# Two-layer diffusion trunk on one core: attention stages and delayed sums placed by a clock of the engines kept while the program is written

## The chip, the cores and the metric

The kernel runs on one core of one Trainium2 chip. The core has TensorE (PE, matrix products into PSUM banks), VectorE (DVE), ScalarE (ACT), GpSimd (POOL) and DMA queues; the queue that brings the weights is issued from SyncE (SP). Each engine takes its own instructions strictly in order and waits at an instruction until its operands are there, so the order in which the program is written decides who waits. The metric is the device time of one execution in microseconds.

## What is computed

Two layers over 256 latent tokens and 256 context tokens of width 1024. Of the reference, cut to what matters:

```python
mx = (silu(c) @ w_ada[l] + b_ada[l]).reshape(bsz, 9, 1, d)     # nine modulation vectors
mc = (silu(c_ctx) @ w_ada[l] + b_ada[l]).reshape(9, d)         # the same of the context
x = x + 0.5 * mx[2] * swiglu(modulate(rmsnorm(x, g[0]), mx[0], mx[1]), w_ffn1_in, w_ffn1_out)
hx = modulate(rmsnorm(x, g[1]), mx[3], mx[4])
p = hx @ w_in                                                   # queries, keys, values, gates
o_a = differential_attention(...)   # 4 heads, "a"
o_b = gated_linear_attention(...)   # 4 heads, both directions, chunks of 64, "b"
o_c = windowed_attention(...)       # 8 heads on 2 key heads, sink logit, "c"
x = x + mx[5] * ((ga*(o_a @ w_br_a) + gb*(o_b @ w_br_b) + gc*(o_c @ w_br_c)) @ w_out)
x = x + 0.5 * mx[8] * swiglu(modulate(rmsnorm(x, g[2]), mx[6], mx[7]), w_ffn2_in, w_ffn2_out)
```

The context goes the same way with `mc`, in layer 1 only as far as the latent tokens read it. The result is the RMS-normed latent stream.

## The kernel before

**Weights.** Every weight is loaded once, 512 KB to a `Unit`, into one of 6 raw buffers `wr`. `split_unit` parts it into a high half `wh` (ACT copies it) and a low half `wl` (DVE subtracts), in a ring of 4 pairs. A product is then three matmuls in place of one: high by high, low by high, high by low (`mm3`, line 112). Activations lie as columns, 512 of them (both streams) in layer 0 and the first FFN of layer 1, 256 in what follows. Nearly all PE work is such a product of `fm_units` (line 411): a unit has two or more *parts*, and a part is a run of 12 matmuls into one bank of PSUM.

**The order.** The program is one flat list that the loop at lines 1380 to 1399 walks. At each part it adds one to `n_part`, first puts in what `later` (line 345) delayed by so many parts, then the part's matmuls, then with `ahead()` the loads and splits that have become possible, and at the end of a unit the work on its result.

**Modulation vectors.** Sixteen vectors (seven of layer 0, all nine of layer 1) are made beside an FFN. `mixed` puts one of eight loads of `w_ada` behind each FFN unit. `ada_step` (line 280) multiplies it on DVE by a column of `sc` into four accumulators `s_t` (two for the last four vectors, of which the context has no use): line 291 for k = 0, line 293 for k = 1 to 7. After k = 7, `later(..., 4)` delays `ada_sum` (line 297) by four parts. `ada_sum` sums each accumulator over its partitions on PE: 32 (or 16) small matmuls against the constant `pick`. `ada_done` then transposes the sums on DVE (line 263) and adds the bias. The two vectors of layer 0 that its first FFN needs are made by matmuls alone and are not touched.

**Mixers.** An attention is a list of items, each a list of stages. An item of "a" or "c" has `s0` (scores, softmax), `s1` (transposes of the probabilities), `s2` (product with the values), and in "a" `s3` (head norm, `finish_head`, line 797: a square on ACT in `s2`, then a sum over partitions by a matmul with `ones_d`, logarithm and exponential on ACT, multiplication on DVE, split into halves). The linear attention has `decay` items ("B", two stages) and `head` items ("b", four stages, with the recurrence over chunks, line 125, in `s1`, and `finish_head` in `s3`). `turns(items, lags)` (line 1010) makes turns of a fixed pattern: turn t holds stage s of item t - lags[s], late stages first. `spread` (line 1069) strews the turns over the parts of the mixer's projections by weights, and at "need a", "need c", "need b", ahead of the first product that reads that attention's result `oh`, it puts in all the turns that are left. Order of groups: a, c, B, b.

Of the kernel before, what the change touches and what calls it, by code (L numbers as in the profile page):

```python
# [16 lines left out]
D = 1024  # L17
# [18 lines left out]
N_SLOT = 69  # L36

LAGS_A0 = (0, 2, 4, 5)
LAGS_C0 = (0, 2, 3)
WEIGHTS0 = (1.0, 1.0, 0.8, 2.0)  # L40
LAGS_A1 = (0, 2, 4, 5)
LAGS_C1 = (0, 2, 3)
# [3 lines left out]
class Ring:  # L46


    def __init__(self, pool, n, prefix):
        self.pool, self.prefix, self.count = pool, prefix, 0  # L50
        self.free = deque(f"{prefix}{i}" for i in range(n))
        self.n = n
        self.low = n
        self.held = {}

    def get(self, dtype=F32, shape=(128, 512)):
# [5 lines left out]
        self.held[id(t)] = (t, tag)  # L62
        return t

# [25 lines left out]

def f32(ap):
    return ap.bitcast(F32)
# [3 lines left out]
def trunk_kernel(ctx: ExitStack, tc: tile.TileContext, a: dict, out: bass.AP, dbg=None):  # L96
# [8 lines left out]
    S = Ring(sp, N_SLOT, "s")  # L105
    P = Ring(pp, 8, "p")


    def mm(o, l, r, start=True, stop=True):
        nc.tensor.matmul(o, l, r, start=start, stop=stop)  # L110
# [7 lines left out]
    def act(o, i, f, **kw):  # L118
        nc.scalar.activation(out=o, in_=i, func=f, **kw)  # L119

    def tt(o, x, y, op):
        nc.vector.tensor_tensor(out=o, in0=x, in1=y, op=op)  # L122

    def stt(o, x, s, y, op0, op1):
        nc.vector.scalar_tensor_tensor(out=o, in0=x, scalar=s, in1=y, op0=op0, op1=op1)  # L125
# [5 lines left out]
    def col(v, name):  # L131
        t = const.tile([128, 1], F32, name=name)
        nc.vector.memset(t, v)
# [12 lines left out]
    nc.vector.memset(ones_d, 1.0 / D)  # L146
    sc = const.tile([128, KD, 32], F32, name="sc")
    nc.vector.memset(sc, 0.0)
    pick = const.tile([128, 2, 32], F32, name="pick")
    nc.vector.memset(pick, 0.0)  # L150
    for s in range(2):
        nc.vector.memset(pick[:, s, s:s + 1], 1.0)
# [14 lines left out]
    def first_loads():  # L167
        cr = raw["c"] = S.get()
        nc.sync.dma_start(out=cr[0:8, 0:128], in_=a["c"].rearrange("o (k p) -> (o k) p", p=128))
        nc.scalar.dma_start(out=cr[8:16, 0:128], in_=a["c_ctx"].rearrange("(k p) -> k p", p=128))  # L170
        nc.scalar.dma_start(out=kf[:, C_ID:C_ID + 128], in_=a["k_f"][:, C_ID:C_ID + 128])
        for l in range(DEPTH):
            r = raw["rows", l] = S.get()
            nc.gpsimd.dma_start(out=r[24:96, 0:128], in_=a["b_ada"][l].rearrange("(k p) -> k p", p=128))
            nc.gpsimd.dma_start(out=r[0:24, 0:128], in_=a["norm_g"][l].rearrange("n (k p) -> (n k) p", p=128))
            nc.gpsimd.dma_start(out=r[96:97, 0:128], in_=a["diff_subln"][l:l + 1, :])
            nc.gpsimd.dma_start(out=r[97:98, 0:128], in_=a["gla_norm"][l:l + 1, :])
            nc.gpsimd.dma_start(out=r[98:106, 0:128], in_=a["final_g"].rearrange("(k p) -> k p", p=128))
# [26 lines left out]
    def tokens(k):  # L205
# [3 lines left out]
        for t in range(4):  # L209
            nc.tensor.transpose(ps[:, t * 128:(t + 1) * 128], raw["t", half, t][:, j * 128:(j + 1) * 128], ident)  # L210
        xt[k] = S.get()
        if k % 2:
            nc.vector.tensor_copy(out=xt[k], in_=ps)
# [7 lines left out]
    def side_loads():  # L221

        nc.sync.dma_start(out=kf[:, 0:C_ID], in_=a["k_f"][:, 0:C_ID])
        for l in range(DEPTH):
            nc.sync.dma_start(out=sink[:, l, :], in_=a["swa_sink"][l:l + 1, :].to_broadcast([128, 8]))
            lp = S.get()
            nc.sync.dma_start(
# [7 lines left out]
            nc.vector.tensor_reduce(out=s, in_=pr, axis=AX.X, op=ALU.add)  # L235
# [25 lines left out]
    def ada_done(l, i, ps, b0=0, nb=KD, streams_=2):  # L261
        tr = S.get()
        nc.vector.transpose(out=tr[:, 0:32 * nb], in_=ps[:, 0:32 * nb])
# [11 lines left out]
        elif i in (2, 8):  # L275
            nc.vector.tensor_scalar_mul(out=m, in0=m, scalar1=0.5)
# [3 lines left out]
    def ada_step(l, i, k, w):  # L280
# [13 lines left out]
        if k == KD - 1:  # L294
            later(lambda: ada_sum(l, i, ns), 4)
# [1156 lines left out]
```

## Time and profile before

| | us |
|---|---|
| median of 3 runs | 2268.08 (2267.97 to 2269.63) |
| the profiled execution, its own time | 2268.44 |
| its span, first to last instruction | 2266.3 |
| PE busy | 2201.1 (97% of the span) |
| DVE busy | 1418.5 (63%) |
| ACT busy | 990.5 (44%) |
| mean granted clock of PE | 0.989 of full speed |

The profiled execution lies 0.4 us above the median and 2.1 us lie outside its span. PE is the engine that is nearly always busy; DVE and ACT have room on the mean, but each is a link in chains that PE waits for. A busy PE may still run at its lower clock, so idle time and granted clock are read together.

### The profile page before, as it was taken

How to read it: one execution, taken by the hardware profiler on the slowest of the kernel's cores; microseconds unless marked ns; L12 is line 12 of the kernel's file. 1: busy time of each engine (PE TensorE's matmuls, PEld its weight loads, DVE VectorE, ACT ScalarE, POOL GpSimd, SP SyncE). 2: the span in 40 equal slices, each digit the busy share in tenths (PEclk: the TensorE clock that was granted, in tenths of full speed). 3: DMA queues.
4: the chain of work that ended last, by engine and by line, in shares of the span. 5: the costliest groups of instructions: out<-in, count | busy, mean ns of one | idle time of the engine just before them, and what ended most of it. 6: DMA issues, size and time to landing. Idle time of an engine off the chain costs nothing.

```text
span 2266.3 us, 32253 instructions
## 1 busy us (share of the span) xinstructions
PE 2201.1 (97%) x12903; PEld 1883.1 (83%) x12903; DVE 1418.5 (63%) x2432; ACT 990.5 (44%) x1701; POOL 17.3 (1%) x40
## 2 busy tenths in 40 slices
PE   7999999998999999999999999999999799998998
PEld 5888888976887788888888898888897688998998
DVE  5677788766465665678776565333366655877655
ACT  4321223666566444432222242222347567664443
POOL 0000000000000000000000000000000000000000
PEclk9999999999999999999999999999999999999999
DMA  8566565331222123356656534333234123356652
GB/s 310 163 188 190 182 193 186 107 88 54 67 65 75 56 66 100 115 167 190 195 183 189 164 123 146 99 97 94 83 96 121 57 84 113 113 164 200 215 185 94
DMA packets 246645, 304.47 MB, mean 134 GB/s; under 512 B 12874, under 2 KB 218180, under 8 KB 246496
## 3 DMA queue, kind: packets, MB, share of 16 engines
q1 hardware_dynamic: 245472, 301.65, 43.1%
q8 instruction: 101, 1.65, 0.3%
q10 hardware_dynamic: 448, 0.59, 0.1%
q14 instruction: 48, 0.39, 0.1%
q0 software_dynamic: 576, 0.18, 0.0%
HBM read 298.19 MB, written 4.19 MB: 133 GB/s over the span
## 4 chain that ended last, share of the span: by engine, by line
PE 84%; DVE 6%; ACT 6%; issue 1%; DMA 1%; SPq 0%; ACTq 0%; DVEq 0%
PE p_t L110 83%; ACT s_t L119 5%; DVE wl L122 2%; DVE s_t L122 1%; DVE s_t L125 1%; ACT wh L119 1%; PE p_t L699 1%; DMA s_t<-in_w_ada_dram 1%; DVE av_s L757 1%; DVE s_t L764 0%; DMA x<-s_t 0%; DVE cv_s L837 0%; SPq L185 0%; DVE av_s L763 0%; PE p_t L623 0%
## 5 line engine op out<-in xcount | busy, mean ns | idle before, releaser
L110 PE MATMUL p_t<-s_t,wh 128*128 128x512 f32 (+1 forms) x6152 | 1638.8, 353 | 2.4 <-ACT wh L119 2.2
L110 PEld LDWEIGHTS p_t<-s_t,wh 128*128 128x128 f32 x6152 | 1086.9, 189 | 171.0 <-issue 9.6
L110 PE MATMUL p_t<-s_t,wl 128*128 128x512 f32 (+2 forms) x3076 | 1046.0, 352 | 0.8 <-DVE wl L122 0.8
L122 DVE TENSOR_TENSOR wl<-wr,wh 128x1024 fp32r<-128x1024 f32 (+2 forms) x423 | 479.1, 1139 | 501.9 <-ACT wh L119 501.1
L119 ACT ACTIVATE wh<-wr 128x1024 fp32r<-128x1024 f32 (+2 forms) x423 | 414.9, 988 | 638.4 <-PE p_t L110 304.0
L110 PEld LDWEIGHTS p_t<-s_t,wl 128*128 128x128 f32 (+1 forms) x3076 | 582.0, 189 | 79.6 <-DVE wl L122 1.3
L119 ACT ACTIVATE s_t<-s_t 128x512 fp32r<-128x512 f32 (+5 forms) x338 | 185.2, 548 | 341.0 <-DVE s_t L122 230.9
L110 PE MATMUL p_t<-s_t,s_t 128*128 128x256 f32 (+4 forms) x2040 | 278.2, 304 | 21.4 <-ACT s_t L119 16.9
L119 ACT ACTIVATE s_t<-p_t 128x512 f32<-128x512 f32 (+6 forms) x464 | 219.3, 490 | 166.5 <-PE p_t L110 103.8
L110 PEld LDWEIGHTS p_t<-s_t,s_t 128*128 128x128 f32 (+2 forms) x2040 | 233.8, 187 | 52.6 <-ACT s_t L119 23.0
L122 DVE TENSOR_TENSOR s_t<-s_t,s_t 128x512 fp32r<-128x512 f32 (+5 forms) x315 | 181.8, 578 | 141.2 <-ACT s_t L119 137.7
L293 DVE SCALAR_TENSOR_TENSOR s_t<-wr,sc,s_t 128x512 f32<-128x512 f32 x392 | 269.0, 746 | 0.0
L122 DVE TENSOR_TENSOR s_t<-s_t,p_t 128x512 f32<-128x512 f32 (+1 forms) x144 | 85.0, 591 | 28.9 <-PE p_t L110 22.2
L110 PE MATMUL p_t<-wh,s_t 128*128 128x512 f32 x256 | 83.7, 399 | 2.8 <-ACT wh L119 2.8
L125 DVE SCALAR_TENSOR_TENSOR s_t<-s_t,mods,s_t 128x256 fp32r<-128x256 f32 (+1 forms) x176 | 70.6, 477 | 10.3 <-ACT s_t L119 10.3
L125 DVE SCALAR_TENSOR_TENSOR s_t<-p_t,mods,s_t 128x256 f32<-128x256 f32 x136 | 60.9, 478 | 21.7 <-PE p_t L110 21.5
L110 PEld LDWEIGHTS p_t<-wh,s_t 128*128 128x128 f32 x256 | 49.3, 193 | 13.3 <-ACT wh L119 3.0
L110 PE MATMUL p_t<-wl,s_t 128*128 128x512 f32 x128 | 51.0, 399 | 0.5 <-DVE wl L122 0.5
L119 ACT ACTIVATE s_t<-p_t,av_s 128x512 f32<-128x512 f32 (+1 forms) x48 | 29.2, 615 | 30.6 <-DVE av_s L758 30.6
L119 ACT ACTIVATE s_t<-s_t,mods 128x256 fp32r<-128x256 f32 x88 | 36.4, 497 | 12.0 <-DVE s_t L125 12.0
L119 ACT ACTIVATE s_t<-s_t,one 128x512 f32<-128x512 f32 (+1 forms) x64 | 40.4, 631 | 2.1
L699 PE MATMUL p_t<-kf,s_t 128*128 128x128 f32 x240 | 36.0, 282 | 0.0
(98 smaller groups left out, 629.7 us busy)
## 6 DMA issues: line engine op xcount, KB each, us to landing
wr<-in_w_ffn_in_dram SPq DMA_DIRECT2D x176, 512.0 KB, 4.3
wr<-in_w_ada_dram SPq DMA_DIRECT2D x128, 512.0 KB, 4.5
wr<-in_w_mix_in_dram SPq DMA_DIRECT2D x108, 512.0 KB, 3.7
wr<-in_w_ffn_out_dram SPq DMA_DIRECT2D x80, 512.0 KB, 3.6
s_t<-in_w_ada_dram SPq DMA_DIRECT2D x32, 256.0 KB, 6.2
wr<-in_w_mix_out_dram SPq DMA_DIRECT2D x16, 512.0 KB, 3.5
wr<-in_w_ffn_out_dram SPq DMA_DIRECT2D x16, 256.0 KB, 2.8
wr<-in_w_br_a_dram SPq DMA_DIRECT2D x8, 512.0 KB, 3.5
```

The lines of the kernel that those rows point to most:

```text
L110: nc.tensor.matmul(o, l, r, start=start, stop=stop)
L119: nc.scalar.activation(out=o, in_=i, func=f, **kw)
L122: nc.vector.tensor_tensor(out=o, in0=x, in1=y, op=op)
L125: nc.vector.scalar_tensor_tensor(out=o, in0=x, scalar=s, in1=y, op0=op0, op1=op1)
L293: eng.scalar_tensor_tensor(out=o, in0=x, scalar=c, in1=o, op0=ALU.mult, op1=ALU.add)
L699: nc.tensor.transpose(pt[:, 128 * t:128 * t + 128], p[:, 128 * t:128 * t + 128], ident)
L757: nc.vector.tensor_reduce(out=v[:, m:m + 1], in_=ps[m][:, 0:nk], axis=AX.X, op=ALU.max)
```

## The change

The fixed turns go. While the program is written, a `Clock` keeps for each engine a time up to which it is taken, and for each tile when it will be there; each engine is wrapped in a `Timed` that books every instruction that goes through it. The costs booked are constants of the code. `later` now takes the tiles that the delayed work waits for and puts it in at the first part at which they are there by that clock (or after 12 parts). The sixteen `ada_sum` go into a deque of their own, `sums`, under the same rule with the accumulators as tiles and 40 parts at most. Mixer items are in a `Group`: at each part a stage goes in if its operands are there, the PSUM banks that it takes are empty and three slots are free; a new `s0` also wants DVE and ACT less than 4.0 us behind. `spread` now only releases items at places given by the same weights, each group a few empty places (`IDLE`) before its "need", and at "need" `Group.finish` puts in whatever stages are left, at once. What an instruction is, and how often it runs, stays the same on every engine.

In `ada_step` the line `eng = nc.vector` (line 387 of the changed kernel) is as it was, not `DVEe`: these products go past the clock.

```diff
-LAGS_A0 = (0, 2, 4, 5)
-LAGS_C0 = (0, 2, 3)
+LATE = 2
+SLACK = 4.0
+
+IDLE = {"a": 5, "c": 3, "B": 1, "b": 3}
...
+    def empty(self, n):
+
+        return len(self.free) >= n and all(
+            self.clock.used.get(b, 0.0) <= self.clock.now["PE"] for b in list(self.free)[:n])
...
         if k == KD - 1:
-            later(lambda: ada_sum(l, i, ns), 4)
+            sums.append((lambda: ada_sum(l, i, ns), tuple(x for a_ in acc for x in a_), "PE", n_part + 40))
...
+    def later(f, *wait, eng="PE", most=12):
+
+        put_off.append((f, wait, eng, n_part + most))
+
+    def is_there(tiles, eng="PE"):
+        return not tiles or clock.at(*tiles) <= max(clock.now["PE"], clock.now[eng])
+
+    def behind(eng):
+        return clock.now[eng] - clock.now["PE"]
+
+    def due():
+        for q in (put_off, sums):
+            while q:
+                f, wait, eng, most = q[0]
+                if n_part < most and not (is_there(wait, eng) and behind("DVE") < SLACK):
+                    break
+                q.popleft()[0]()
+        for g in list(live):
+            g.step()
...
+    class Group:
...
+        def step(self, force=False):
...
+            for i in range(self.begun):
+                s = self.at[i]
+                if s == len(self.items[i]) or i and self.at[i - 1] <= s:
+                    continue
+                f, wait, banks = self.items[i][s]
+                if not force:
+                    if not is_there(wait() if wait else ()) or not P.empty(banks) or len(S.free) < 3:
+                        continue
+                    late = self.begun - i > LATE
+                    if s == 0 and not (fresh and (late or behind("DVE") < SLACK and behind("ACT") < SLACK)):
+                        continue
+                f()
+                self.at[i] += 1
...
+        def finish(self):
+            self.begun = len(self.items)
+            while not self.over:
+                self.step(True)
...
-            todo = deque((g, t, wt) for g, (ts, wt) in groups.items() for t in ts)
+            todo = deque()
+            for name, (g, idle, wt) in groups.items():
+                todo.extend((name, g.start if i < len(g.items) else lambda: None, wt) for i in range(len(g.items) + idle))
...
+                        out_.append(groups[g][0].finish)
...
-            "a": (and_then(turns(a_items(), lags_a), free_a), weights[0]),
+            "a": (Group(a_items(), free_a), IDLE["a"], weights[0]),
...
         elif p[0] == "part":
             n_part += 1
-            while put_off and put_off[0][0] < n_part:
-                put_off.popleft()[1]()
+            due()
```

The order moves at two kinds of places. The first is each of the sixteen sums. On PE, around the sum of layer 1's vector 0 (`pick` rows; `p_t`... `wh` rows are an FFN's products), the rows before are:

```order
L110 MATMUL p_t359_9183<-s_t639_8173,wh153_9095 128x512
L110 MATMUL p_t359_9183<-s_t642_8178,wh153_9095 128x512
L110 MATMUL p_t361_9239<-s_t684_8860,pick_83 32x128 x4
L110 MATMUL p_t361_9239<-s_t686_8862,pick_83 32x128 x4
L110 MATMUL p_t361_9239<-s_t685_8861,pick_83 32x128 x4
L110 MATMUL p_t361_9239<-s_t687_8863,pick_83 32x128 x4
L110 MATMUL p_t360_9196<-s_t632_8162,wh153_9095 128x512
```

The sum stands between the two parts of `wh153`. After, the same stretch of PE's queue is:

```order
L159 MATMUL p_t358_9112<-s_t639_8173,wh151_9017 128x512
L159 MATMUL p_t358_9112<-s_t642_8178,wh151_9017 128x512
L159 MATMUL p_t359_9183<-s_t685_8881,pick_83 32x128 x4
L159 MATMUL p_t359_9183<-s_t687_8883,pick_83 32x128 x4
L159 MATMUL p_t359_9183<-s_t686_8882,pick_83 32x128 x4
L159 MATMUL p_t359_9183<-s_t688_8884,pick_83 32x128 x4
L159 MATMUL p_t360_9203<-s_t620_8142,wh152_9055 128x512
```

The sum stood inside the products of `wh153`; now it stands at the end of those of `wh151`, three parts of 12 matmuls earlier. On DVE, the same sum: the last products into the accumulators (L293, in the changed kernel L393, with wr234), then splits and the transpose of the sum, the rows before are:

```order
L122 TENSOR_TENSOR s_t700_9168<-s_t696_9085,s_t699_9167 128x512
L293 SCALAR_TENSOR_TENSOR s_t684_8860<-wr234_9051,sc_81,s_t684_8860 128x512
L293 SCALAR_TENSOR_TENSOR s_t685_8861<-wr234_9051,sc_81,s_t685_8861 128x512
L293 SCALAR_TENSOR_TENSOR s_t686_8862<-wr234_9051,sc_81,s_t686_8862 128x512
L293 SCALAR_TENSOR_TENSOR s_t687_8863<-wr234_9051,sc_81,s_t687_8863 128x512
L122 TENSOR_TENSOR wl155_9180<-wr241_9177,wh155_9179 128x1024
L291 TENSOR_SCALAR s_t701_9209<-wr236_9091,sc_81 128x512
L291 TENSOR_SCALAR s_t702_9210<-wr236_9091,sc_81 128x512
L291 TENSOR_SCALAR s_t703_9211<-wr236_9091,sc_81 128x512
L291 TENSOR_SCALAR s_t704_9212<-wr236_9091,sc_81 128x512
L122 TENSOR_TENSOR wl156_9222<-wr243_9219,wh156_9221 128x1024
L263 STREAM_TRANSPOSE s_t706_9256<-p_t361_9239 128x256
```

Behind the last products come the next vector's first four, two splits, and only then the transpose. After, DVE's rows from the same gate product on are:

```order
L159 TENSOR_TENSOR s_t700_9168<-s_t696_9085,s_t699_9167 128x512
L393 SCALAR_TENSOR_TENSOR s_t685_8881<-wr234_9051,sc_81,s_t685_8881 128x512
L393 SCALAR_TENSOR_TENSOR s_t686_8882<-wr234_9051,sc_81,s_t686_8882 128x512
L393 SCALAR_TENSOR_TENSOR s_t687_8883<-wr234_9051,sc_81,s_t687_8883 128x512
L393 SCALAR_TENSOR_TENSOR s_t688_8884<-wr234_9051,sc_81,s_t688_8884 128x512
L159 TENSOR_TENSOR wl155_9180<-wr241_9177,wh155_9179 128x1024
L159 STREAM_TRANSPOSE s_t701_9200<-p_t359_9183 128x256
L159 TENSOR_TENSOR mods1_90<-s_t701_9200,cols1_88 128x16
L391 TENSOR_SCALAR s_t702_9229<-wr236_9091,sc_81 128x512
```

The products into the accumulators keep their place behind the FFN's gate (the first row); the transpose moved up past the next vector's first products and one split.

The second kind is the mixers. On PE, at the end of layer 1's mixer, ahead of the first product of the third branch (`wh317`), which reads all heads' results, the rows before are:

```order
L110 MATMUL p_t641_17159<-s_t917_13719,wh316_17033 128x256
L110 MATMUL p_t641_17159<-s_t920_13724,wh316_17033 128x256
L110 MATMUL p_t641_17159<-s_t923_13729,wh316_17033 128x256
L110 MATMUL p_t641_17159<-s_t926_13734,wh316_17033 128x256
L110 MATMUL p_t642_17216<-s_t1160_16771,wh317_17089 128x256
L110 MATMUL p_t642_17216<-s_t1160_16771,wl317_17090 128x256
```

The branch stands behind a projection's products and nothing else. After, PE's rows ahead of the same branch are:

```order
L159 MATMUL p_t638_17161<-s_t1065_15401,s_t1131_16325 128x128
L159 MATMUL p_t639_17162<-s_t1065_15401,s_t1131_16325 128x128
L159 MATMUL p_t640_17194<-s_t1181_17171,s_t1059_15341 128x128 x2
L159 MATMUL p_t640_17194<-s_t1039_15107,s_t1182_17176 128x64 x2
L159 MATMUL p_t640_17194<-s_t1181_17171,s_t1060_15349 128x128 x2
L159 MATMUL p_t640_17194<-s_t1039_15107,s_t1182_17176 128x64 x2
L159 MATMUL p_t641_17205<-s_t1184_17203,ones_d_79 128x256
L159 MATMUL p_t642_17216<-s_t1163_16867,wh317_17002 128x256
L159 MATMUL p_t642_17216<-s_t1163_16867,wl317_17003 128x256
```

Before, the last head was through 48 projection matmuls ahead of the branch; after, its stages `s1` (p_t638, p_t639), `s2` (p_t640) and `s3` (`ones_d`) stand directly ahead of the branch, put in by `Group.finish`.

## Rows read from the trace of the kernel before

**Rows 1.** The page: busy time and instructions by engine; the chain that ended last.

```profile
PE 2201.1 (97%) x12903; PEld 1883.1 (83%) x12903; DVE 1418.5 (63%) x2432; ACT 990.5 (44%) x1701; POOL 17.3 (1%) x40
...
PE 84%; DVE 6%; ACT 6%; issue 1%; DMA 1%; SPq 0%; ACTq 0%; DVEq 0%
```

**Rows 2.** Waits of PE over the span: us in total, times, longest us.

```profile
PE p_t L110 <- ACT s_t L119: 29.3, 17, 5.9
...
PE p_t L653 <- ACT s_t L119: 3.6, 2, 2.6
```

**Rows 3.** Stretches: us, busy (x instructions) by engine, granted clock, DMA share, GB/s.

```profile
1000.00:1250.00 250.00, 250.00 (x1250) 205.22 (x1249) 187.94 (x272) 65.94 (x78) 0.00 (x0) 1.00 0.62 192
...
1450.00:1500.00 50.00, 50.00 (x222) 41.43 (x221) 17.22 (x22) 10.77 (x11) 0.00 (x0) 1.00 0.33 100
...
2112.00:2140.00 28.00, 28.00 (x236) 28.00 (x235) 16.74 (x23) 12.49 (x18) 0.00 (x0) 1.00 0.67 213
...
470.00:600.00 130.00, 116.36 (x571) 93.03 (x571) 77.50 (x157) 81.94 (x181) 2.71 (x5) 0.96 0.23 66
1714.00:1990.00 276.00, 254.09 (x1771) 221.66 (x1770) 185.34 (x390) 177.87 (x365) 4.96 (x13) 0.97 0.33 97
```

**Rows 4.** Timeline of DVE: start, duration, [idle before]; last products of four vectors.

```profile
115.04 2.73 DVE L293 SCALAR_TENSOR_TENSOR s_t<-wr,sc,s_t 128x512 f32<-128x512 f32 x4
...
382.96 2.74 DVE L293 SCALAR_TENSOR_TENSOR s_t<-wr,sc,s_t 128x512 f32<-128x512 f32 x4
...
1062.03 0.69 DVE L122 TENSOR_TENSOR s_t<-s_t,s_t 128x512 fp32r<-128x512 f32 x1 [0.70 <-ACT s_t L119]
1062.64 2.73 DVE L293 SCALAR_TENSOR_TENSOR s_t<-wr,sc,s_t 128x512 f32<-128x512 f32 x4
...
2107.71 1.41 DVE L293 SCALAR_TENSOR_TENSOR s_t<-wr,sc,s_t 128x512 f32<-128x512 f32 x2
```

**Rows 5.** Timeline of PE: the sums of the same four vectors.

```profile
123.34 1.08 PE L110 MATMUL p_t<-s_t,pick 128*32 128x128 f32 x32
...
386.42 1.08 PE L110 MATMUL p_t<-s_t,pick 128*32 128x128 f32 x32
...
1068.06 1.08 PE L110 MATMUL p_t<-s_t,pick 128*32 128x128 f32 x32
...
2110.58 0.65 PE L110 MATMUL p_t<-s_t,pick 128*32 128x128 f32 x16
```

**Rows 6.** Timeline of PE: first and last of nine waits of 1.98 us or more.

```profile
26.29 2.08 PE L110 MATMUL p_t<-s_t,s_t 128*128 128x512 f32 x4 [1.98 <-ACT s_t L119]
...
2057.52 0.79 PE L110 MATMUL p_t<-s_t,s_t 128*128 128x256 f32 x2 [4.88 <-ACT s_t L119]
```

**Rows 7.** Stretches at three of the seven falls of the clock that followed, columns as above.

```profile
24.00:34.00 10.00, 8.02 (x29) 5.55 (x29) 9.07 (x22) 5.50 (x12) 0.00 (x0) 0.66 1.06 381
...
1769.00:1773.00 4.00, 4.00 (x24) 4.00 (x22) 2.90 (x7) 1.00 (x4) 0.00 (x0) 0.57 0.44 131
...
2056.00:2067.00 11.00, 8.93 (x40) 8.31 (x41) 9.20 (x20) 6.74 (x13) 0.00 (x0) 0.53 0.55 188
```

**Rows 8.** Timeline, layer 1's mixer: a head's recurrence and the end of another head.

```profile
1953.40 0.77 DVE L958 COPY_PREDICATED s_t<-kf,p_t 128x256 f32<-128x256 uint32 x2
...
1954.12 0.40 DVE L972 MEMSET s_t<- 64x128 f32 x2
...
1954.55 0.61 DVE L979 COPY s_t<-p_t 64x128 f32<-64x128 f32 x2
...
1955.19 4.51 DVE L125 SCALAR_TENSOR_TENSOR s_t<-s_t,s_t,p_t 64x128 f32<-64x128 f32 x12
...
1962.77 0.46 ACT L119 ACTIVATE s_t<-p_t,eps 128x256 f32<-128x256 f32 x1
...
1963.26 0.42 ACT L119 ACTIVATE s_t<-s_t 128x256 f32<-128x256 f32 x1
...
1965.52 0.48 DVE L125 SCALAR_TENSOR_TENSOR s_t<-p_t,cols,s_t 128x256 f32<-128x256 f32 x1
```

More of the change, by code (lines that the diff above doesn't have):

```diff
@@ L88, in __getitem__, with __init__, tile, cells @@
         return self.views[k // 2][p, k % 2, c]
+class Clock:
+    def __init__(self):
+        self.now = {e: 0.0 for e in ("PE", "ACT", "DVE", "POOL", "SP", "LOAD")}
+        self.ready, self.used, self.home, self.fresh = {}, {}, {}, set()
+        self.stall = []
+    def tile(self, t, home):
+        name = t.tensor.name
+        self.home[name] = home
+        self.fresh.add(name)
+    def cells(self, aps):
+        out = []
+        for a in aps:
+            lo = a.offset % max(a.ap[0][0], 1)
+            hi = lo + sum((n - 1) * abs(st) for st, n in a.ap[1:])
+            out += [(a.tensor.name, i) for i in range(lo // 128, min(hi // 128 + 1, lo // 128 + 16))]
+        return out
+    def at(self, *aps):
+        return max(self.ready.get(n, 0.0) for n in self.cells(aps))
+    def run(self, eng, cost, outs, ins, lag=0.1, load=False):
+        begin = self.now[eng]
+        for n in self.cells(ins):
+            begin = max(begin, self.ready.get(n, 0.0))
+        for n in self.cells(outs):
+            begin = max(begin, self.ready.get(n, 0.0) if eng != "PE" else 0.0)
+            if n[0] in self.fresh:
+                self.fresh.discard(n[0])
+                begin = max(begin, self.used.get(self.home[n[0]], 0.0))
+        if eng == "PE" and begin > self.now[eng] + 0.3:
+            self.stall.append((round(self.now[eng], 1), round(begin - self.now[eng], 2), outs[0].tensor.name, [i.tensor.name for i in ins]))
+        end = begin + cost
+        self.now[eng] = end
+        if load:
+            end = max(end, self.now["LOAD"]) + 1.75
+            self.now["LOAD"] = end
+            end += 2.0
+        for n in self.cells(outs):
+            self.ready[n] = end + lag
+        for a in outs + ins:
+            h = self.home.get(a.tensor.name, a.tensor.name)
+            self.used[h] = max(self.used.get(h, 0.0), end + lag)
@@ new lines, with __init__, __getattr__, call @@
+class Timed:
+    def __init__(self, eng, name, clock):
+        self.eng, self.name, self.clock = eng, name, clock
+    def __getattr__(self, op):
+        f = getattr(self.eng, op)
+        if op in ("preload_act_table_set",):
+            return f
+        def call(*args, **kw):
+            r = f(*args, **kw)
+            aps = [(k, v) for k, v in [(str(i), v) for i, v in enumerate(args)] + list(kw.items()) if hasattr(v, "tensor")]
+            outs = [v for k, v in aps if k in ("0", "out", "accum_out")]
+            ins = [v for k, v in aps if k not in ("0", "out", "accum_out")]
+            n = max(math.prod(v.shape[1:]) for _, v in aps) if aps else 1
+            self.clock.run(self.name, self.cost(op, n, outs, ins), outs, ins, load=op == "dma_start")
+            return r
+        return call
+    def cost(self, op, n, outs, ins):
+        if op == "dma_start":
+            return 0.06
+        if self.name == "PE":
+            if op == "transpose":
+                return 0.11 * math.prod(ins[0].shape[1:]) / 128
+            c = math.prod(ins[1].shape[1:])
+            if ins[0].dtype == F32R:
+                return c / 2400 + 0.0133
+            k, m = ins[0].shape[0], math.prod(ins[0].shape[1:])
+            part = 0.3 if m <= 32 else 0.55 if m <= 64 or k <= 64 and k != 33 else 1.0
+            return part * (4 * c / 2400 + 0.007)
+        if self.name == "ACT":
+            return 0.2 + 0.0008 * n
+        if op == "scalar_tensor_tensor":
+            return 0.2 + 0.00106 * n
+        return 0.14 + 0.00102 * n
@@ L104, in trunk_kernel @@
     ctx.enter_context(tc.manual_schedule())
-    S = Ring(sp, N_SLOT, "s")
-    P = Ring(pp, 8, "p")
+    clock = Clock()
+    PEe, ACTe, DVEe = Timed(nc.tensor, "PE", clock), Timed(nc.scalar, "ACT", clock), Timed(nc.vector, "DVE", clock)
+    POOLe, SPe = Timed(nc.gpsimd, "POOL", clock), Timed(nc.sync, "SP", clock)
+    S = Ring(sp, N_SLOT, "s", clock)
+    P = Ring(pp, 8, "p", clock)
     def mm(o, l, r, start=True, stop=True):
-        nc.tensor.matmul(o, l, r, start=start, stop=stop)
+        PEe.matmul(o, l, r, start=start, stop=stop)
     def mm3(o, lh, ll, rh, rl, start, stop):
@@ L566, in turn @@
                 S.put(r)
-            later(turn)
+            later(turn, r, q, eng="DVE")
             return q
@@ L573, in done @@
                 q = rope(ps, nq)
-                later(lambda: dst.update({b + m: made(q)}), 2 + m)
+                later(lambda: dst.update({b + m: made(q)}), q, eng="ACT")
             return done
@@ L643, in keys @@
                     S.put(q)
-                later(keys, 2)
+                later(keys, q, eng="ACT")
             else:
@@ L786, in s3 @@
                         finish_head(o_ps[h], box["sq"], subg, None, "a", h)
-                return [s0, s1, s2, s3]
+                return [(s0, lambda: [x for t in ([aq[h]] if h in aq else []) + (list(ak[h]) if h in ak else []) for x in t], 2),
+                        (s1, lambda: [box["p"]], 1), (s2, lambda: [box["t"]], 1 + 2 * first),
+                        (s3, lambda: [box["sq"]] if last else [], 1)]
             items = []
```

189 lines of the change are left out of this document (103 added, 86 removed).

## Prediction, written before the changed kernel was run

> **What bounds the kernel now.** I read the busy shares first, then the chain that ended last, then who waited for whom, then the stretches. PE is busy 2201.1 of 2266.3 us and holds 84% of the chain [rows 1]: the time is PE's own work plus what PE waits or runs at its lower clock. Where does that lie? In FFN stretches, not at all: from 1000 to 1250 PE is busy 250.00 of 250 us at clock 1.00, DVE 187.94 us [rows 3]. It lies in the mixers. From 470 to 600 PE is idle 130 - 116.4 = 13.6 us and loses (1 - 0.96) x 130 = 5.2 us to the clock; from 1714 to 1990 it is 276 - 254.1 = 21.9 and 0.03 x 276 = 8.3 us [rows 3]. Together 49 us, which is all that a better order of the mixers could ever give. The releaser of most of it is ACT: 29.3 us in 17 waits of one kind [rows 2].
>
> **Part one: the sums.** The diff says that a sum goes in when its accumulators are there by the clock. The products into them are issued through an engine that isn't wrapped, so for the clock they take no time and the accumulators are there at once: the order shows each of the sixteen sums at the very next part, four parts sooner. What that costs is a sum of rows. Between the new place and the old lie 36 matmuls of 512 columns; 222 of these start in 50 us [rows 3], 0.2252 us each, so PE reaches the sum 8.1 us sooner. DVE's products keep their place. At layer 1's vector 0 they end at 1062.64 + 2.73 = 1065.37 and the sum starts at 1068.06 [rows 4, 5]: the slack was 2.7 us and 8.1 are taken. PE arrives near 1059.96 and waits. The sum can begin with what the third of four products made and do half of its 1.08 us [rows 5] meanwhile, which takes 0.54 - 0.1 (my estimate of the hop) = 0.44 off: 8.1 - 2.69 - 0.44 = 4.97 us of wait. The same for all: the slacks of the twelve with four accumulators, in order, are 5.56, 6.26, 6.18, 7.25, 6.10, 6.28, 0.72, 2.81, 2.69, 6.05, 4.53 and 2.65 (first, seventh and ninth of them in [rows 4, 5]), 57.1 in all, and the waits 12 x (8.1 - 0.44) - 57.1 = 34.8 us. Three with two accumulators (slacks 4.65, 4.36, 5.09; 0.23 off each) give 3 x 7.87 - 14.1 = 9.5. The last is among matmuls of 256 columns: 236 in 28.00 us [rows 3], 48 lie between, 5.7 us, slack 2110.58 - 2109.12 = 1.46 [rows 4, 5], wait 4.0. Sum: **48.3 us**.
>
> Why doesn't DVE simply get ahead, since it is idle a quarter of the time? Because its queue is tied to PE: the row ahead of the products at 1062.03 is a gate product of the same FFN unit that waited 0.70 us for ACT [rows 4], and that chain begins with PE's result. A PE that is 5 us later makes DVE 5 us later. So the wait comes back at each vector and isn't paid once. For the first six vectors the tie is looser (their slack is 5.6 to 7.3 us and the wait 0.4 to 2.1): from them alone 8.3 us may vanish. What is queued behind the waiting sum is PE itself, all of it; nothing else covers a wait there, since PE was at 250.00 of 250.
>
> **Part two: the clock.** Nine waits of PE of 1.98 us or more stand in the trace, the first and the last of them in [rows 6], and seven of them were followed at once by a stretch at half clock, three of them in [rows 7]: (1 - 0.66) x 10 = 3.4 us, 0.43 x 4 = 1.7 and 0.47 x 11 = 5.2 us lost. The seven sum to 22.2 us, or 2.5 us for each of the nine. Of the sixteen waits above ten are 2 us or longer (2.1, 6.9, 4.9, 5.0, 3.1, 5.0, 3.2, 3.5, 2.8, 4.0). 10 x 2.5 = **25 us**. Bounds: 0 if the clock stays up in an FFN, 10 x 5.2 = 52 if each costs what the dearest did.
>
> That the rows of granted clock mean what they say has its own check: at 1769 to 1773 PE is busy 4.00 of 4 us and starts 24 matmuls, where 28.00 us at clock 1.00 hold 236, 33.7 in 4 us [rows 3, 7]. The Trainium skill, TensorE: Matmul & The Clock Gate, "Seeing it yourself", warns that the clock's events in a trace were seen to be unreliable and asks for a cross-check; if they were wrong here this term would be 0 and the sum 2315, but the count of matmuls speaks for the rows.
>
> **Part three: the mixers.** Their instructions are the same, in an order that follows the clock, and what is left at a "need" is forced in. By the order that happens at five places. The dearest is the end of layer 1's mixer: the last head's stages s1, s2, s3 and another's s3 directly ahead of the branch that reads them, where before 48 matmuls of projection and more lay between. The chain there, from rows of the same work [rows 8]: 0.77 + 0.40 + 0.61 + 4.51 = 6.3 us on DVE for the recurrence, then on PE, ACT, PE, ACT, DVE, ACT: products and square about 1.3 (an estimate), logarithm 0.46, exponential 0.42, product 0.48, a second product and the high half about 0.42 each, and some 1.4 us of hops (an estimate), 11.2 us that PE waits. In layer 1's "need a" two items' s2 and s3 are forced: the ACT-DVE end of that chain with a neighbour's softmax ahead of it on ACT, 6.5 to 8.7, I take 7.6. In layer 0's "need a" five stages of two items: 4.9. At the two "need c" one or two stages: 1.4 and 1.6. In sum 27 us, where before PE waited for none of them. Against it stand the waits that the fixed turns had, 35.5 us idle. About 5 of these lie ahead of layer 1's mixer, at its first splits (1714 to 1724), and stay; of the rest I keep 5, as a stage waits for its operands now. Clock: four long waits at 2.5, 10 us. New loss 27 + 10 + 10 = 47 against 49: **-2 us**. This is the least certain term; its bounds are -40 (all but the 5 at the splits and a little clock gone) and +25 (the forced places each with the dearest fall of the clock, and the old waits half kept).
>
> **The sum** is made against the profiled execution's own 2268.4 us, 0.4 above the median: 2268.4 + 48.3 + 25 - 2 = 2339.7; against the median 2339.
>
> **Rivals.**
> - *The clock stays up* in FFN stretches, because a lone wait isn't a mixer's cluster of waits: two of the nine waits had no fall behind them. Sum without the 25: 2315. Against it: the wait ahead of 2057.52 stands at an FFN's start and cost the most. 15%.
> - *The forced ends cost more than I take*: each is a queue of four engines and delays the next group, so the mixers lose 20 to 25 us more than before: 2362. For it: the order shows head stages of one item issued back to back, with nothing of PE between. 14%.
> - *The mixers do what the change says*: few waits are left, -40, while the sums cost as worked out: 2301. Against it: five forced places that the order shows. 6%.
> - *Faster*: DVE does get ahead after the first wait, since it has a quarter of its time free; the sums then cost next to nothing, and the mixers lose 17 in place of 49: 2268 - 32 = 2236. It decides by the tie: if the gate product ahead of the last products waited for something that isn't PE's result, a late PE would free DVE. The row at 1062.03 shows ACT as releaser, which stands in PE's chain. 6%.
> - *The sums hidden in that way, the mixers even*: 2266, within 0.2%. 4%.
> - My forecast, 2339, with 2318 to 2362 of its own: 55%.
>
> **How the numbers follow.** The likeliest case gives 2339. Low end: the case of 2301 is half in at 2303. High end: 2366 holds the costly forced ends with a few us to spare. Left out are the two cases at or under 2268 (10%), half of 2301 (3%) and some 5% above, under 2 in 10. A measurement of this kernel can tell some 0.2% (4.5 us) from no change. Faster by more than that 0.06, within 0.04, slower 0.90.
>
> **What would show it.** In the trace of the changed kernel each sum with `pick` should be released by a DVE product into an accumulator, with PE idle ahead of it: about 7 us at the seventh (near 390 us), about 5 at the eighth, ninth and twelfth, 0.4 to 2 at the first six. A stretch of FFN such as 1000 to 1250 should hold 15 to 20 us of idle PE and a granted clock under 1.00. In layer 1's mixer the wait at the end, ahead of the branch of the heads, should be the longest of all, near 11 us with a DVE and ACT chain in it. I am wrong in part one if sums start without idle time ahead, in part two if the granted clock in FFN stretches stays 1.00, in part three if mixers show under 25 or over 60 us of loss.

## The result, and the profile after

The changed kernel takes 2350.53 us (median of 4 runs, 2348.69 to 2352.95) against 2268.02 in the same comparison: ratio 1.0364, 95% interval 1.0346 to 1.0382. It is slower by 82 us; 2339 was forecast, 2303 to 2366 the range. Its page, the same parts as [rows 1]:

```profile
span 2348.5 us, 32261 instructions
...
PE 2227.7 (95%) x12903; PEld 1896.7 (81%) x12903; DVE 1421.1 (61%) x2432; ACT 989.3 (42%) x1701; POOL 17.0 (1%) x40
...
PE 71%; DVE 12%; ACT 8%; DMA 5%; issue 3%; SPq 0%; ACTq 0%; DVEq 0%
```

The instructions are the same in number. PE is idle 121 us instead of 65 and busy 27 us longer at the same work. Some 10 us of these 27 are the matmuls of the sums (25.4 us in place of 15.6, taken apart below); the rest goes with the clock, 0.975 of full speed in place of 0.989. The chain holds less PE and twice the DVE. The waits of PE, where [rows 2] stood:

```profile
PE p_t L159 <- ACT s_t L159: 43.8, 22, 7.8
PE p_t L159 <- DVE s_t L393: 39.8, 22, 5.6
PE p_t L159 <- DVE s_t L159: 17.0, 12, 4.6
```

The second row is new. L393 is the line of the products into the accumulators, and nothing but a sum waits for them. The FFN stretch that was full in [rows 3], and the 15 us around the seventh sum:

```profile
1000.00:1250.00 250.00, 233.12 (x1117) 188.30 (x1116) 175.25 (x253) 57.55 (x68) 0.00 (x0) 0.95 0.55 168
...
385.00:400.00 15.00, 8.77 (x53) 6.49 (x53) 7.93 (x13) 1.31 (x2) 0.00 (x0) 0.66 0.48 141
```

Of 250 us, PE is idle 16.9, and its granted clock is 0.95. The sums themselves, in PE's timeline (first row the first vector, second and third the seventh, then the ninth, to be read against [rows 5]):

```profile
116.36 1.09 PE L159 MATMUL p_t<-s_t,pick 128*32 128x128 f32 x24 [0.90 <-DVE s_t L393]
...
390.59 0.65 PE L159 MATMUL p_t<-s_t,pick 128*32 128x128 f32 x8 [5.56 <-DVE s_t L393]
391.92 1.51 PE L159 MATMUL p_t<-s_t,pick 128*32 128x128 f32 x24 [0.67 <-DVE s_t L393]
...
1088.25 0.66 PE L159 MATMUL p_t<-s_t,pick 128*32 128x128 f32 x8 [3.52 <-DVE s_t L393]
1089.58 1.51 PE L159 MATMUL p_t<-s_t,pick 128*32 128x128 f32 x24 [0.67 <-DVE s_t L393]
```

Where the rest of the 82 us is, no view says by itself. The weight matmuls come in the same order in both kernels, 9612 of them, so the start of the n-th in one trace less its start in the other is the delay up to that place. A difference of two columns is what the stretch between cost. For the profiled execution of each kernel told of below (us later than in the kernel before, negative is sooner):

| kernel | behind layer 0's first FFN | behind layer 0's mixer | ahead of layer 1's mixer | behind it | end |
|---|---|---|---|---|---|
| changed kernel | 16.2 | 16.9 | 58.9 | 76.4 | 82.2 |
| e1_sums_back | -0.1 | 0.8 | 0.9 | 19.1 | 18.8 |
| e2_sums_early | 17.6 | 18.7 | 65.5 | 66.9 | 73.0 |
| e4_sums_one_part | 6.3 | 6.3 | 19.4 | 19.4 | 22.5 |
| e5_sums_filled | 29.0 | 27.4 | 85.8 | 85.8 | 93.0 |
| e5b_filled_short | 14.4 | 15.4 | 47.8 | 47.7 | 50.9 |
| e6_late_rule | 0.8 | 3.9 | 4.0 | 15.1 | 14.9 |
| e7_heads_fixed | -0.4 | 0.1 | 0.1 | 8.2 | 7.3 |
| e9_nothing_forced | -0.1 | -12.2 | -12.2 | -1.6 | -1.6 |
| e10_layer0_timed | -0.1 | -13.6 | -13.6 | -12.6 | -13.1 |
| e11_layer1_a_timed | -0.5 | -12.6 | -12.5 | -4.8 | -5.4 |

In the changed kernel the stretches with sums cost 16.2 + 42.0 + 5.8 = 64 us, layer 0's mixer 0.7 and layer 1's 17.5.

### The profile page after: what moved, and what is told of

Its sections match the earlier page's. It is cut to its first block, busy times and chain, and to the rows that moved or that the text cites. A ratio compares the mean times of both kernels' runs of the same rounds, so it can differ in the third digit from the quotient of the medians.

```text
span 2348.5 us, 32261 instructions
## 1 busy us (share of the span) xinstructions
PE 2227.7 (95%) x12903; PEld 1896.7 (81%) x12903; DVE 1421.1 (61%) x2432; ACT 989.3 (42%) x1701; POOL 17.0 (1%) x40
## 4 chain that ended last, share of the span: by engine, by line
PE 71%; DVE 12%; ACT 8%; DMA 5%; issue 3%; SPq 0%; ACTq 0%; DVEq 0%
PE p_t L159 71%; ACT s_t L159 6%; DVE s_t L159 4%; DVE s_t L393 4%; DVE wl L159 3%; ACT wh L159 2%; DMA wr<-in_w_ffn_in_dram 2%; DMA wr<-in_w_ffn_out_dram 1%; DMA s_t<-in_w_ada_dram 1%; DVE av_s L159 1%; DVE cv_s L159 0%; DMA x<-s_t 0%; DMA s_t<-in_ctx_dram 0%; DVE s_t L391 0%; SPq L159 0%
## 5 line engine op out<-in xcount | busy, mean ns | idle before, releaser
L159 PE MATMUL p_t<-s_t,wh 128*128 128x512 f32 (+1 forms) x6152 | 1658.5, 355 | 12.9 <-ACT s_t L159 10.4
L159 PEld LDWEIGHTS p_t<-s_t,wh 128*128 128x128 f32 x6152 | 1094.9, 190 | 186.4 <-ACT s_t L159 13.9
L159 PE MATMUL p_t<-s_t,s_t 128*128 128x256 f32 (+5 forms) x2040 | 271.0, 302 | 29.9 <-ACT s_t L159 19.2
L159 ACT ACTIVATE s_t<-p_t 128x512 f32<-128x512 f32 (+5 forms) x464 | 219.6, 490 | 185.1 <-PE p_t L159 124.1
L159 PEld LDWEIGHTS p_t<-s_t,s_t 128*128 128x128 f32 (+3 forms) x2040 | 232.3, 186 | 57.4 <-ACT s_t L159 28.1
L393 DVE SCALAR_TENSOR_TENSOR s_t<-wr,sc,s_t 128x512 f32<-128x512 f32 x392 | 269.1, 747 | 0.0
L159 DVE TENSOR_TENSOR s_t<-s_t,s_t 128x256 f32<-128x256 f32 (+5 forms) x315 | 181.7, 577 | 133.3 <-ACT s_t L159 129.6
L159 DVE SCALAR_TENSOR_TENSOR s_t<-p_t,mods,s_t 128x256 f32<-128x256 f32 x136 | 60.9, 479 | 22.5 <-PE p_t L159 22.5
L159 PE MATMUL p_t<-kf,s_t 128*128 128x128 f32 (+3 forms) x459 | 61.6, 292 | 12.7 <-DVE s_t L159 4.9
L159 PEld LDWEIGHTS p_t<-kf,s_t 128*128 128x128 f32 (+3 forms) x459 | 49.7, 151 | 25.5 <-issue 10.0
L159 PE MATMUL p_t<-s_t,pick 128*32 128x128 f32 x448 | 25.4, 337 | 40.0 <-DVE s_t L393 39.8
L159 PEld LDWEIGHTS p_t<-wh,s_t 128*128 128x128 f32 x256 | 48.1, 188 | 14.4 <-ACT s_t L159 4.4
L159 PEld LDWEIGHTS p_t<-s_t,pick 128*32 128x32 f32 x448 | 11.8, 125 | 54.1 <-DVE s_t L393 51.3
```

What stands on the lines that cost most here:

```text
L159: r = f(*args, **kw)
L393: eng.scalar_tensor_tensor(out=o, in0=x, scalar=c, in1=o, op0=ALU.mult, op1=ALU.add)
```

## Experiments on the sums

**e1_sums_back** undoes the new place of the sums and leaves the mixers as changed:

```diff
-            sums.append((lambda: ada_sum(l, i, ns), tuple(x for a_ in acc for x in a_), "PE", n_part + 40))
+            sums.append((lambda: ada_sum(l, i, ns), n_part + 4))
...
-        for q in (put_off, sums):
+        while sums and sums[0][1] < n_part:
+            sums.popleft()[0]()
+        for q in (put_off,):
```

> The changed kernel, with the sixteen sums put in four parts after the last products again, as before the change; the mixers stay placed by the clock. Theory A (the sums' place costs what the delay of the weight matmuls shows in the three stretches that hold them, 16.6 + 42.1 + 5.4 = 64 us, and the mixers the other 18): 2350.5 - 64 = 2286 us, no PE wait on a DVE product left, granted clock 1.00 from 1000 to 1250. Rival B (the mixers' order is what costs, and the sums' waits are made up by DVE elsewhere): 2330 or more.

2287.61 us, 1.0083 of the kernel before (1.0068 to 1.0098). The row of waits on L393 is gone, and the delay is under 1 us up to layer 1's mixer. So 63 of the 82 us are the sums' place, and 19 the mixers.

**e2_sums_early** moves the sums alone, in the kernel before:

```diff
-            later(lambda: ada_sum(l, i, ns), 4)
+            later(lambda: ada_sum(l, i, ns), 0)
```

> The kernel before, with nothing changed but that each sum goes in at the next part instead of four parts later. Theory A: 2268 + 64 = 2332 us, with about 40 us of PE waits on DVE products and some 8 falls of the clock. Rival B: within 10 us of 2268.

2340.33 us, 1.0311 (1.0296 to 1.0327): 71 us, 7 more than expected. In this kernel the last sum but one goes 48 matmuls sooner, 36 in the changed one, and the stretch with it cost 7.6 us in place of 2.9. The other 2 to 3 us are within what the runs of this kernel differ by (2335.3 to 2341.4, with a mean clock of 0.978 to 0.974).

**e4_sums_one_part** has a 1 in that place.

> The kernel before, with each sum delayed by one part instead of four: 24 matmuls (5.4 us) sooner than before for fourteen of the sixteen. Theory A with DVE tied to PE: a wait at a vector is 5.4 less its slack less 0.44, so only the vectors with little slack wait (the seventh 4.2 us, the eighth, ninth and twelfth about 2.2 each, the others 0 to 0.8; 13 us in all) and, with three or four falls of the clock at 1.7 to 3.4 us, the time is 2268 + 13 + 9 = 2290. If DVE were free to run ahead, each wait but the first would go and the time would be within 5 us of 2268; if each sum cost a fixed amount wherever it stands ahead of its old place, about 2268 + 2/3 of 64 = 2311.

2291.97 us, 1.0105 (1.0088 to 1.0121), where 2290 was expected, with 14.9 us of waits on the products in place of 13. In its trace the first six sums, which had the most slack, wait for nothing, the seventh waits 3.6 us and the ninth 1.7. So the price of a sum isn't fixed, and it doesn't vanish after the first: it is the matmuls given up less the slack, vector by vector.

**e5_sums_filled and e5b_filled_short** separate the idle time from the clock. Both are the kernel with early sums and idle matmuls ahead of each (the numbers here are those of e5b):

```diff
+FILL = deque([2, 1, 2, 1, 2, 1, 13, 9, 9, 2, 5, 13, 6, 7, 11, 8])
...
         ps = P.get()
+        for _ in range(FILL.popleft()):
+            mm(ps[:, 0:256], ones_d, kf[:, 0:256])
```

> As the sums at the next part in the kernel before, but ahead of each sum PE does idle matmuls (ones_d by a constant, 128x256 fp32, some 0.215 us each by the rows of before), as many as fill the wait that I worked out (1 to 32, 207 in all). They add nothing to the result. Theory A on the clock (it falls because PE idles): the waits stay in length, about 45 us of added matmuls or waits, but no fall of the clock follows a sum: 2268 + 45 = 2313. Rival C (the loss beyond the waits is not the idle time's doing, but that of the moved DVE work or of the sum itself): 2332 or more, as without the fill.

2363.99 us, 1.0419 (1.0403 to 1.0434). The size of the fill was wrong: the numbers in the code add up to 217 matmuls, not 207, and these are 434 records that fill 96.3 us, twice what I had reckoned. So the time answers to the fill and tells nothing on the sum. The clock answers: ahead of the sums PE was never idle, and from 1000 to 1250 it was busy 250.00 of 250 us at clock 1.00.

> The kernel with early sums alone, again with idle matmuls ahead of each sum that add nothing to the result, now counted from the trace: one takes 0.445 us (two records of 0.22), and their number per sum (1 to 13, 92 in all) is the wait measured with early sums alone, 45 us in all, divided by that. So PE has about the same time taken at each sum, busy in place of idle. Theory A on the clock (idle time ahead of a sum is what lets it fall): granted clock 1.00 in the FFN stretches, 2268 + 41 of fill + a few us of waits left = 2311 to 2316. Rival C (the time beyond the waits belongs to the early sums whether PE idles or not): 2335 to 2341, as measured with early sums alone.

2320.17 us, 1.0229 (1.0214 to 1.0245): 4 us above what theory A gave and 15 below rival C. PE's groups for the fill and the sums in this kernel (instructions | busy us, mean ns | idle us before), its stretch from 1000 to 1250, and then both of early sums without a fill:

```profile
L112 PE MATMUL p_t<-kf,ones_d 128*128 128x256 f32 x184 | 42.3, 379 | 0.0
...
L112 PE MATMUL p_t<-s_t,pick 128*32 128x128 f32 x448 | 20.5, 281 | 5.7 <-DVE s_t L295 5.2
```

```profile
1000.00:1250.00 250.00, 248.30 (x1226) 203.22 (x1225) 179.04 (x258) 59.14 (x69) 0.00 (x0) 1.00 0.54 173
```

```profile
L110 PE MATMUL p_t<-s_t,pick 128*32 128x128 f32 x448 | 25.4, 336 | 44.1 <-DVE s_t L293 43.9
```

```profile
1000.00:1250.00 250.00, 232.13 (x1107) 187.31 (x1106) 173.46 (x252) 57.25 (x67) 0.00 (x0) 0.95 0.52 168
```

The same sums in the same places, 42.3 us of idle work in place of 38 us of idling, and the kernel is 20 us faster, with the clock at 1.00 where it was 0.95. So the clock's share of early sums is about 20 us (up to 24, as the fill takes 4 us more than the idling that it replaces), and it falls because PE idles; the other 47 to 51 are the wait as such.

## Experiments on the mixers

All start from e1_sums_back (2287.61). Its two mixers, each over its whole length, where [rows 3] has a part; first the kernel before and then this one, layer 0 above layer 1:

```profile
470.00:760.00 290.00, 276.13 (x1457) 218.36 (x1456) 165.27 (x368) 179.39 (x383) 3.76 (x7) 0.98 0.23 67
1714.00:2030.00 316.00, 294.09 (x2103) 261.61 (x2102) 211.55 (x430) 206.37 (x418) 4.96 (x13) 0.97 0.36 105
```

```profile
470.00:760.00 290.00, 273.96 (x1455) 217.70 (x1455) 167.06 (x370) 177.41 (x381) 3.65 (x7) 0.98 0.23 68
1714.00:2049.00 335.00, 300.45 (x2109) 269.19 (x2108) 214.35 (x434) 209.33 (x421) 4.82 (x13) 0.94 0.34 101
```

Layer 0: 16 us idle in place of 14. Layer 1: 34.5 in place of 21.9, and 0.06 of 335 us lost to the clock in place of 0.03 of 316. The longest waits of the mixers stand where stages are forced. These rows are the changed kernel's, and the waits at the same places of e1_sums_back agree to 0.01 us: the first is ahead of layer 0's branch "a", then come layer 1's "a" (two head norms), "c" (an s2), and "b" (four rows, the recurrence of the last head between them on DVE).

```profile
627.53 1.23 PE L159 MATMUL p_t<-s_t,s_t 128*128 128x128 f32 x4 [4.81 <-ACT s_t L159]
...
1921.66 1.22 PE L159 MATMUL p_t<-s_t,ones_d 128*128 128x256 f32 x2 [7.83 <-ACT s_t L159]
...
2002.32 2.24 PE L159 MATMUL p_t<-s_t,s_t 128*64 128x128 f32 x15 [3.94 <-ACT s_t L159]
...
2061.54 1.19 PE L159 MATMUL p_t<-s_t,s_t 128*128 128x128 f32 x4 [3.58 <-DVE s_t L159]
...
2062.74 4.51 DVE L159 SCALAR_TENSOR_TENSOR s_t<-s_t,s_t,p_t 64x128 f32<-64x128 f32 x12
...
2067.30 2.82 PE L159 MATMUL p_t<-s_t,s_t 128*128 128x64 f32 x12 [4.57 <-DVE s_t L159]
...
2070.59 1.22 PE L159 MATMUL p_t<-s_t,ones_d 128*128 128x256 f32 x2 [0.47 <-ACT s_t L159]
...
2074.25 0.58 PE L159 MATMUL p_t<-s_t,wh 128*128 128x256 f32 x1 [1.16 <-ACT s_t L159]
```

The last head was held back by the rule of the clock: a first stage wants DVE less than 4.0 us behind, unless two later items of its group are released too, which the last two items never have. **e6_late_rule** drops that for a group whose items are all released:

```diff
-                    late = self.begun - i > LATE
+                    late = self.begun - i > LATE or self.begun == len(self.items)
```

> The kernel with timed mixers and the sums back at their place (2287.6), with one more clause: once all items of a group are released, a first stage may go in although DVE is over 4.0 us behind. By the program, the last head's s0 and s1 then go in ahead of layer 1's need b and only its s2 and s3 are forced (before that: s1, s2, s3 of it and s3 of another); the forced stages at the other needs stay. Theory M (stages forced in directly ahead of a branch are what the mixers lose): the waits of 9.8 us and the fall of the clock behind them shrink by more than half, 2277 to 2281. Rival N (the loss lies in the order of the stages elsewhere, the end only takes over waits): within 4 us of 2287.6.

2283.80 us, 1.0069 (1.0054 to 1.0084). That is 3.8 us, at the edge of what rival N allows and short of the 6.6 that theory M wanted. At the end 1.78, 3.61 and 1.16 us of wait are left of 9.8, so they did not shrink by half. The table shows more than the total: layer 1's mixer costs 11.1 us in place of 18.2, and layer 0's, where the clause works too, 3.1 in place of 0.9. So the gain in layer 1 is 7 us, as theory M has it, and a part of it is lost elsewhere, as rival N has it.

**e7_heads_fixed** puts the heads into fixed turns, by a class that plays the old turns where the group released its items:

```diff
-            "b": (Group(heads, lambda: (free_b(), free_la()), gates), IDLE["b"], weights[3]),
+            "b": (Turns(heads, (0, 1, 2, 3), lambda: (free_b(), free_la()), gates), 0, weights[3]),
```

> The kernel with timed mixers and the sums back at their place (2287.6), with the head items of the linear attention in the fixed turns of the kernel before; differential and windowed attention and the decays stay placed by the clock. The delay of the weight matmuls put 21.9 us of that kernel's 18.6 us net loss at the end of layer 1's mixer. Theory M: that goes, and 2287.6 - 20 = 2267.5 us is left, no longer different from the kernel before. Rival N: the wait moves to another place, 2280 or more.

2275.10 us, 1.0029 (1.0017 to 1.0040): 12.5 of 20 us, between the two theories. The wait at the end went, but the windowed attention's forced end, a 3.94 us wait before, now stands behind a head's recurrence on DVE and the sigmoids on ACT:

```profile
1943.09 4.51 DVE L159 SCALAR_TENSOR_TENSOR s_t<-s_t,s_t,p_t 64x128 f32<-64x128 f32 x12
...
1947.63 0.38 ACT L159 ACTIVATE s_t<-p_t 128x256 f32<-128x256 f32 x1 [5.76 <-DVE s_t L159]
...
1950.76 0.47 PE L159 MATMUL p_t<-s_t,s_t 128*64 128x128 f32 x1 [7.36 <-ACT s_t L159]
```

So both theories hold a part: the forced ends make up much of the loss, and taking one away lengthened another. That it does because the stages draw on the same two engines fits these rows; no run shows it by itself.

**e9_nothing_forced** changes four rules:

```diff
-SLACK = 4.0
+SLACK = 8.0
-IDLE = {"a": 5, "c": 3, "B": 1, "b": 3}
+IDLE = {"a": 8, "c": 6, "B": 1, "b": 3}
...
+                    late = self.begun - i > LATE or self.begun == len(self.items)
+                    if s == 0 and any(g is not self and g.first for g in live[:live.index(self)]):
+                        continue
```

> The kernel with timed mixers and the sums back at their place (2287.6), with four rules changed: SLACK 8.0, IDLE 8, 6, 1, 3 (groups released earlier), the clause for last items, and no first stage of another group while the differential attention has stages left. By the program nothing is forced in at any need but the last head's s3. Theory M: without the forced ends (some 26 us of waits and falls of the clock at the four places) and with the waits that timed stages save elsewhere, 2287.6 - 26 = 2262, under the kernel before. Rival N (a stage that goes in earlier waits for its operands where it stands, since DVE and ACT are no faster): 2275 to 2290.

2266.76 us, 0.9990 (0.9981 to 1.0000): 21 us under e1_sums_back, about level with the kernel before, and between the two theories, nearer to M. The four rules were not tried one by one. By the delays layer 0's mixer is 12.1 us faster than in the fixed order and layer 1's 10.6 slower. **e10_layer0_timed** takes the first and leaves the second: timed groups in layer 0, fixed turns for all four groups in layer 1.

> Layer 0's mixer as in the kernel in which nothing is forced (timed, with the four changed rules), layer 1's mixer in the fixed turns of the kernel before, sums at their old place. In the trace of that kernel the weight matmuls behind layer 0's mixer came 12.2 us sooner than in the kernel before and layer 1's mixer gave back 10.6. Theory M (each mixer's gain or loss is its own): 2269 - 12 = 2257 us, faster than both. Rival N (what a timed order saves in one place comes back in the next): 2264 to 2269.

2255.85 us, 0.9943 (0.9928 to 0.9957). It beats both kernels, as theory M had it. Its mixer in layer 0, to be read against that row of the kernel before:

```profile
470.00:745.00 275.00, 269.00 (x1442) 217.04 (x1441) 164.59 (x367) 174.50 (x377) 3.58 (x7) 0.99 0.24 72
```

In layer 0 PE idles 6.0 us in place of 13.9, at clock 0.99 in place of 0.98. **e11_layer1_a_timed** times the differential attention in layer 1 as well.

> As the kernel with only layer 0's mixer timed, and in layer 1 the differential attention timed too, with decays, heads and windowed attention there in fixed turns; two head norms of the differential attention are forced at its need. If layer 1's loss is in its heads and in the windowed attention: 2257 to 2260. If it is in the differential attention itself, whose items stand thick in the short parts of 256 columns and which is forced at its need: 2262 to 2270.

2263.80 us, 0.9976 (0.9966 to 0.9986): 8 us more than without. By the delays, layer 1's mixer costs 1.0 us with all four groups in fixed turns, 7.7 with the differential attention timed and 10.6 with all four timed. So most of what the timed order loses in layer 1 is in the differential attention there, if the losses of the groups add up. Why the same rules win with parts of 512 columns and lose with 256 is not settled; a part in which to hide a chain is half as long there, and I have no run that changes that alone.

Not tried on the chip: the changed kernel with the products into the accumulators booked like all the rest. By the program its clock then sees DVE some 40 us behind in the FFN, holds each sum for its full 40 parts, and the accumulators that are kept so long leave too few slots for the rest. So the runs show what the sums' early place costs; that the missing bookings put them there is read from the code and the order.

## Why the prediction was right

**The sums' waits** (forecast 48.3 us, about 45 measured). In the changed kernel PE idled 40.0 us at the sums' matmuls, and that includes the second wait inside a sum (0.67 us at the seventh and the ninth). The matmuls took 25.4 us in place of 15.6 in the kernel before. They come in two pieces now, behind the first and behind the third product, and eight of the sums run in part at half clock: the second piece takes 1.51 us at the seventh where it takes 1.09 at the first. At clock 1.00, in e5b_filled_short, the sums in two pieces took 20.5 us, so 4.9 of the 9.8 belong to the wait and the rest to the clock. At the ninth sum DVE's products ended at 1087.45 + 2.73 = 1090.18 and PE had come at 1084.73: DVE still had 5.45 us to go, against 8.1 - 2.69 = 5.41 by the rows of before. The first six, with the loose tie, cost some 7 us where 8.3 were worked out. The sum used an estimate of 0.1 us for the hop from DVE to PE, for which no row of before was given; at the ninth sum PE started 0.05 us after the product that it waited for. The sums' group before and after (instructions | busy us, mean ns | idle us before), then the rows of the ninth on ACT and on DVE:

```profile
L110 PE MATMUL p_t<-s_t,pick 128*32 128x128 f32 x448 | 15.6, 276 | 0.0
...
L159 PE MATMUL p_t<-s_t,pick 128*32 128x128 f32 x448 | 25.4, 337 | 40.0 <-DVE s_t L393 39.8
```

```profile
1081.24 1.06 ACT L159 ACTIVATE wh<-wr 128x1024 fp32r<-128x1024 f32 x1 [4.01 <-DMA wr<-in_w_ffn_in_dram]
```

```profile
1077.26 1.23 DVE L159 TENSOR_TENSOR wl<-wr,wh 128x1024 fp32r<-128x1024 f32 x1 [0.68 <-ACT wh L159]
1078.41 2.74 DVE L393 SCALAR_TENSOR_TENSOR s_t<-wr,sc,s_t 128x512 f32<-128x512 f32 x4
1082.34 1.23 DVE L159 TENSOR_TENSOR wl<-wr,wh 128x1024 fp32r<-128x1024 f32 x1 [1.20 <-ACT wh L159]
...
1086.84 0.69 DVE L159 TENSOR_TENSOR s_t<-s_t,s_t 128x512 fp32r<-128x512 f32 x1 [0.70 <-ACT s_t L159]
1087.45 2.73 DVE L393 SCALAR_TENSOR_TENSOR s_t<-wr,sc,s_t 128x512 f32<-128x512 f32 x4
```

**The tie** of DVE to PE held: PE idled at fifteen of the sixteen sums, and the delay by one part gave 2291.97 us where 2290 was forecast from the tie. But it is longer than I told. In the rows above DVE waits for ACT, which waited for a weight load to land, ahead of the ninth vector's gate products. The chain that ended last shows how the load hangs on DVE and where PE comes in:

```profile
1073.85 2.74 DVE s_t L393 x4
...
1076.61 4.53 DMA wr<-in_w_ffn_in_dram
...
1081.24 1.07 ACT wh L159
...
1089.58 24.94 PE p_t L159 x120
```

DVE's products free a raw buffer, the next load goes into it, ACT and DVE split it, and only then come the gate products, whose own PE result was there; behind the sum PE holds the chain for 25 us. So the row at 1062.03, from which I argued, is one of two ties. These loads are also why the chain now holds 5% DMA.

**The clock** (forecast 25 us, about 18 measured). The direction was right, shown by the fill. Nine of the sixteen sums wait 2.5 us or longer, where ten of 2 us or longer were forecast, and eight of them come with a fall. The term was too large: the sums cost 63 us in the changed kernel and about 45 of it is wait; in early sums alone the fill gave 20 of 71. I had charged half the length of each fall, but a fall begins while PE still waits, and that part of it costs nothing. At the seventh sum the clock fell at 387.5 and the wait ended at 390.6 (columns as in [rows 3]):

```profile
387.50:390.60 3.10, 0.01 (x1) 0.01 (x2) 3.10 (x5) 0.00 (x0) 0.00 (x0) 0.50 0.21 34
390.60:397.70 7.10, 6.43 (x42) 4.64 (x43) 2.73 (x6) 0.00 (x0) 0.00 (x0) 0.50 0.68 207
```

The Trainium skill (TensorE: Matmul & The Clock Gate, "Seeing it yourself") cautions that the clock's events in a trace were seen to be unreliable. Here they agree with the time, which fell by 20 us where the fill took the falls away.

**The mixers** (forecast -2 us, +18.6 measured) is the step that failed, though within its bounds of -40 to +25. The forced ends were right in place and size: 27 us forecast, in e1_sums_back and the changed kernel about 28 (layer 0: 4.8 + 0.7 and 1.1; layer 1: 7.8, 3.9, and 3.6 + 4.6 + 0.5 + 1.2). The end of layer 1's mixer was not the longest single wait, as I had said: its 9.9 us (11.2 forecast) come in four pieces, and the longest is the head norms' 7.83. What failed are the two terms beside the forced ends. I left 10 us for waits elsewhere, and there are 16.0 + 34.5 - 28 = 22; and I took 10 us for the clock, where layer 1 alone lost 0.06 x 335 = 20 and layer 0 0.02 x 290 = 6. The longest fall of the trace, 17 us at half clock, began in layer 1's last forced end. In the forecast's own way of counting that is 28 + 22 + 26 = 76 us of loss against 47, over the 60 that it named as its sign of being wrong. These terms are 28 us too small and the time shows 20.6, as more of the falls than before lies inside waits (15 us at half clock in place of 3) and costs nothing there.

The errors had opposite signs: some 10 us too much for the sums (3 in the waits, 7 in the clock) and 20.6 too few in the mixers. It is luck that the forecast of 2339 came as near as 11 us.

Of the rivals, the costly forced ends came nearest in size, but for another reason than it gave: the ends cost what I took, and the other waits and the clock were dearer. The clock did not stay up, and DVE did not run free.

## What to carry to other kernels

A delay in program order that looks idle can be the slack of a slower engine. Its price when removed is the work given up less the slack, to be paid at every recurrence if the slower engine is tied to the faster one, and again in clock if the wait is long. A planner's clock that leaves out some instructions calls ready what isn't; and with a rule "as soon as it is there" what is left at a deadline is forced in as one uncovered chain, so it is worth starting early enough that nothing is left (21 us here, though layer 1 still did better in its fixed turns).

## What was not expected of the hardware

Filling a wait with useless matmuls, 42.3 us of them, made the kernel 20 us faster than idling there, because the granted clock from 1000 to 1250 stayed at 1.00 rather than 0.95. One 128x256 product in fp32 is two records of about 0.22 us, 0.445 us in all, seen only when 217 of them took 96.3 us. The same doubling holds for a sum: its 32 (or 16) records in the rows are 16 (or 8) matmuls of the program.
